# A gated recurrence's factor computed without the square of a, and its exchanged copy by GpSimd

## Chip, cores, metric

One Trainium2 chip; the program runs on one of its cores. The metric is device microseconds of one execution, as the median of the runs shown.

## What is computed

Two layers of a hybrid backbone over 256 context and 256 latent tokens of width 2048. Each layer projects the tokens to 7184 columns and feeds three groups: a bidirectional gated recurrence (RG-LRU, 1024 channels), windowed attention with 8 heads, and a bidirectional state space scan (SSD, 16 heads). A projection back to 2048 columns and a residual close the layer. The change lies in the recurrence:

```python
def rglru_scan(xc, w_a, b_a, w_x, b_x, lam, h0, reverse):
    ...
    r = jax.nn.sigmoid(jnp.einsum('blhi,hij->blhj', xb, w_a.astype(jnp.float32)).reshape(bsz, L, W) + b_a)
    i = jax.nn.sigmoid(jnp.einsum('blhi,hij->blhj', xb, w_x.astype(jnp.float32)).reshape(bsz, L, W) + b_x)
    log_a = -LRU_C * r * jax.nn.softplus(-lam.astype(jnp.float32))
    a = jnp.exp(log_a)
    b = jnp.sqrt(-jnp.expm1(2.0 * log_a)) * (i * xf)
    ...
    h = linear_scan(a, b, reverse)
```

It runs once per direction. The gates' weights are block diagonal: 16 blocks of 64 channels.

## The kernel before

**Work of the matmuls.** Activations lie with channels on the 128 partitions and the 512 tokens along the row. A projection to 128 columns is one PSUM tile `acc` of 128 x 512, summed over 16 blocks of the input. So that fp32 accuracy is kept, every weight piece is split into `hi` and `lo` (`blocks`, L228): a piece of 256 KB comes by DMA into one of five `raw` buffers, ScalarE copies it to `hi` (L237), VectorE subtracts to get `lo` (L238), and each of its four blocks gives three matmuls (`mm3`, L242). There are four buffers for `hi` and four for `lo`. TensorE's order of work is written by hand; the other engines' order is set by a scheduler at build time, and each engine works its own queue strictly in that order.

**Order of a layer.** Projections run in the order of `body` (L72): columns for the state space scan first, then in turn for the eight channel tiles of the recurrence `lx` (its input, always 512 tokens) and `lg` (its gate; 512 tokens in layer 0, only the 256 latent ones in layer 1), then the rest. After each projection its follow-up work is started as a generator; parts of it that need TensorE are put between the matmuls once a clock that counts matmul time has gone on by the amount in the table `WAIT`. While the tiles of the recurrence are projected, the state space scan (`ssd_core`; L1119 to L1191) also runs.

**One channel tile of the recurrence** (`lru_x`, L688). ScalarE and VectorE do a convolution of four taps over `acc` into `xc` (L460, three times L466). The gates' matmuls work on quadrants of 64 x 64 and need the two halves of `xc` also exchanged: ScalarE makes the copy `xsw`, two halves of 64 x 512 (L694). Then, for each direction: eight small matmuls into two PSUM tiles `mx` (four of these are shared by everybody); ScalarE takes the two gates out by Tanh (L712), giving `tr` and `ti`; Tanh of log a into `tl` (L717); Exp, which gives a (L718); Square of a into `la2` (L720). VectorE multiplies (a squared + 1) into `tl` (L721) and makes (ti + 1) x xc (L722). With both directions done ScalarE takes the root of `tl` in one operation of 128 x 1024 (L724), before which it loads another activation table. GpSimd multiplies it into `ti` (L727), VectorE runs the recurrences (L730; L733 and L735 backward), GpSimd adds the directions (L739) and multiplies by the output gate (L749), and the result is stored to DRAM. Since tanh(log a) = (a^2 - 1)/(a^2 + 1), the product of L721 is a^2 - 1.

`xc`, `la2`, the gate `lgt` and other roles share the four buffers of tag `td`.

Of the kernel before, what the change touches and what calls it, by code (L numbers as in the profile page):

```python
# [10 lines left out]
AF = mybir.ActivationFunctionType  # L11
ALU = mybir.AluOpType
AX = mybir.AxisListType

P = 128
# [124 lines left out]
class Kernel:  # L140
# [526 lines left out]
    def lru_begin(self, l):  # L667
        nc = self.nc
        o = PARAMS["lam"][0]
        ng = self.t([P, 16], "nlam", 1)  # L670
        nc.vector.tensor_scalar(out=ng, in0=self.prm[:, o:o + 16], scalar1=-1.0, scalar2=None, op0=ALU.mult)
        sp = self.softplus(ng, 16, "lsp")
        self.s4 = self.t([P, 16], "s4", 1)
        nc.vector.tensor_scalar(out=self.s4, in0=sp, scalar1=-4.0, scalar2=None, op0=ALU.mult)
        self.gb = self.t([P, 32], "gbh", 1)
        o = PARAMS["gab"][0]
        nc.vector.tensor_scalar(out=self.gb, in0=self.prm[:, o:o + 32], scalar1=0.5, scalar2=None, op0=ALU.mult)
        self.gws = [self.gate_weights(l, 0)]
        self.lruD = self.dram([8, P, 512], "lruD")
# [8 lines left out]
    def lru_x(self, l, m, px):  # L688
        nc = self.nc
        xc = self.t([P, 512], "xc")  # L690
        self.conv(xc, px, lambda tap: self.par("lcw", tap * 8 + m), self.par("lcb", m), 2)
        xs = self.t([P, 512], "xsw")
        for r, o in ((0, 64), (64, 0)):
            nc.scalar.activation(out=xs[r:r + 64], in_=xc[o:o + 64], func=AF.Copy)  # L694
        gw = self.gws.pop(0)
        if m < 7:
            self.gws.append(self.gate_weights(l, m + 1))
        yield self.wait("lx")
        ab = []
        tl = self.t([P, 2, 512], "ltl", 1)  # L700
        for d in range(2):
            if d:
                yield self.wait("lx2")
            th = []
            pg = [self.mx() for _ in range(2)]
            for r, c in ((0, 0), (64, 64), (0, 64), (64, 0)):
                x = xc if r == c else xs
                self.mm(pg[r // 64][c:c + 64], gw[r:r + 64, int(r != c), 2 * d + r // 64], x[r:r + 64], pos=(r, c),
                        side=4)
            for g in range(2):  # L710
                t = self.t([P, 512], f"lt{g}", 2)
                nc.scalar.activation(out=t, in_=pg[g], func=AF.Tanh, scale=0.5,  # L712
                                     bias=self.gb[:, 16 * g + 8 * d + m:16 * g + 8 * d + m + 1])
                th.append(t)
            tr, ti = th
            s4 = self.s4[:, 8 * d + m:8 * d + m + 1]
            nc.scalar.activation(out=tl[:, d], in_=tr, func=AF.Tanh, scale=s4, bias=s4)  # L717
            nc.scalar.activation(out=tr, in_=tr, func=AF.Exp, scale=s4, bias=s4)  # L718
            a2 = self.t([P, 512], "la2", 1)
            nc.scalar.activation(out=a2, in_=tr, func=AF.Square)  # L720
            nc.vector.scalar_tensor_tensor(out=tl[:, d], in0=a2, scalar=1.0, in1=tl[:, d], op0=ALU.add, op1=ALU.mult)  # L721
            nc.vector.scalar_tensor_tensor(out=ti, in0=ti, scalar=1.0, in1=xc, op0=ALU.add, op1=ALU.mult)  # L722
            ab.append((tr, ti))
        nc.scalar.activation(out=tl, in_=tl, func=AF.Sqrt, scale=-0.0625, bias=self.eps["s"])  # L724
        hs = []
        for d, (tr, ti) in enumerate(ab):
            nc.gpsimd.tensor_tensor(out=ti, in0=ti, in1=tl[:, d], op=ALU.mult)  # L727
            h = self.t([P, 512], f"lh{d}", 2)
            if d == 0:
                nc.vector.tensor_tensor_scan(out=h, data0=tr, data1=ti, initial=0.0, op0=ALU.mult, op1=ALU.add)  # L730
            else:
                r = lambda x, s: x[:, s:s + 256][:, ::-1]
                nc.vector.tensor_tensor_scan(out=r(h, 0), data0=r(tr, 0), data1=r(ti, 0), initial=0.0, op0=ALU.mult,  # L733
                                             op1=ALU.add)
                nc.vector.tensor_tensor_scan(out=r(h, C), data0=r(tr, C), data1=r(ti, C), initial=h[:, 0:1],  # L735
                                             op0=ALU.mult, op1=ALU.add)
            hs.append(h)
        s = C if l else 0
        nc.gpsimd.tensor_tensor(out=hs[0][:, s:], in0=hs[0][:, s:], in1=hs[1][:, s:], op=ALU.add)  # L739
        self.lru_h[m] = hs[0]  # L740
# [536 lines left out]
```

## Time and profile before

| what | value |
|---|---|
| runs | 1833.20, 1832.97, 1830.13 us; median 1832.97 |
| profiled execution, own time | 1829.47 us |
| its span | 1827.5 us |
| busy: TensorE | 1765.5 us (97%) |
| busy: VectorE | 1407.4 us (77%) |
| busy: ScalarE | 973.3 us (53%) |
| busy: GpSimd | 214.7 us (12%) |
| granted clock of TensorE, mean | 0.991 |

The span runs from the first to the last instruction in the trace; the time holds 2 us more around it. PE is TensorE, PEld its weight loads, DVE is VectorE, ACT is ScalarE, POOL is GpSimd. The shares are means over the whole program: ScalarE's work is concentrated in the two stretches of the recurrence, 225 to 495 us (layer 0) and 1290 to 1495 us (layer 1).

### The profile page before, as it was taken

The page shows a single profiled execution, that of the slowest core. Times are in us where ns is not written, and L with a number is a line of the kernel's source. Part 1 is how long each engine was busy: PE and PEld are TensorE (multiplying, and loading weights), DVE is VectorE, ACT ScalarE, POOL GpSimd, SP SyncE. Part 2 cuts the span into 40 slices and gives each one's busy share as a digit, 9 for nine tenths or more (in the row PEclk, how much of TensorE's full clock was granted, in tenths as well). Part 3 has the DMA queues.
Part 4 walks back from the last instruction along what each step waited for, and adds up shares of the span by engine and source line. Part 5 has one row for each costly group of instructions (what it writes and reads, how often), then busy time and mean ns, then how long its engine had stood idle before and what let it go on. Part 6 is the DMA issues. An engine that isn't in the chain of part 4 may idle for free.

```text
span 1827.5 us, 30170 instructions
## 1 busy us (share of the span) xinstructions
PE 1765.5 (97%) x10522; PEld 1453.4 (80%) x10522; DVE 1407.4 (77%) x3117; ACT 973.3 (53%) x1798; POOL 214.7 (12%) x179
## 2 busy tenths in 40 slices
PE   7999999999999999999999999999989999999999
PEld 4677876667778778887888887888767788999999
DVE  4447769898899778899999536877688785788665
ACT  4324578688523354556232235545688863678443
POOL 0000111111210021211000021010021130121000
PEclk9999999999999999999999999999999999999999
DMA  9982333434675545556766433455243564554655
GB/s 364 389 292 66 124 104 102 122 122 146 220 221 180 179 150 185 178 182 221 238 220 222 158 122 107 133 185 168 96 138 107 179 214 142 182 178 155 217 185 179
DMA packets 186344, 322.99 MB, mean 177 GB/s; under 512 B 19121, under 2 KB 44625, under 8 KB 185553
## 3 DMA queue, kind: packets, MB, share of 16 engines
q1 hardware_dynamic: 186192, 321.09, 54.2%
q8 instruction: 82, 1.34, 0.3%
q14 instruction: 70, 0.57, 0.1%
HBM read 310.38 MB, written 10.63 MB: 176 GB/s over the span
## 4 chain that ended last, share of the span: by engine, by line
PE 72%; DVE 9%; issue 7%; ACT 7%; DMA 3%; POOL 1%; SPq 0%; ACTq 0%; DVEq 0%; POOLq 0%
PE acc L174 55%; PE mx L174 13%; PE ada L174 3%; DVE lo L238 2%; PE mx L170 2%; DMA bc<-acsD 1%; ACT hi L237 1%; DVE ada L380 1%; DVE araw L380 1%; ACT lt L712 1%; DVE lh L730 1%; DMA araw<-in_adaw_dram 1%; DVE xc L466 1%; DVE ee L1165 1%; ACT ww L1167 1%
## 5 line engine op out<-in xcount | busy, mean ns | idle before, releaser
L174 PE MATMUL acc<-u,hi 128*128 128x512 f32 (+1 forms) x4800 | 1277.4, 355 | 3.9 <-ACT u L452 3.1
L174 PEld LDWEIGHTS acc<-u,hi 128*128 128x128 f32 x4800 | 837.1, 190 | 149.0 <-issue 32.6
L174 PE MATMUL acc<-u,lo 128*128 128x512 f32 (+1 forms) x2400 | 842.4, 351 | 6.9 <-DVE lo L238 6.7
L237 ACT ACTIVATE hi<-raw 128x512 fp32r<-128x512 f32 x640 | 397.8, 628 | 544.4 <-PE acc L174 420.8
L238 DVE TENSOR_TENSOR lo<-raw,hi 128x512 fp32r<-128x512 f32 x640 | 457.9, 718 | 184.6 <-ACT hi L237 172.7
L174 PEld LDWEIGHTS acc<-u,lo 128*128 128x128 f32 x2400 | 455.5, 190 | 71.9 <-DVE lo L238 11.7
L380 DVE SCALAR_TENSOR_TENSOR araw<-araw,adac 128x512 f32<-128x512 f32 x256 | 183.2, 716 | 6.9 <-DMA araw<-in_adaw_dram 4.1
L380 DVE SCALAR_TENSOR_TENSOR ada<-araw,adac 128x512 f32<-128x512 f32 x192 | 141.6, 738 | 13.0 <-DMA adac<-condD 7.0
L174 PE MATMUL mx<-u,hi 128*128 128x512 f32 (+1 forms) x320 | 99.7, 395 | 0.0
L1077 DVE SCALAR_TENSOR_TENSOR X<-acc,mod,X 128x256 f32<-128x256 f32 x144 | 65.0, 478 | 39.5 <-PE acc L174 39.4
L727 POOL TENSOR_TENSOR lt<-lt,ltl 128x512 f32<-128x512 f32 x32 | 45.5, 1443 | 326.2 <-ACT ltl L724 305.3
L868 POOL TENSOR_SCALAR prob<-prob,qrs 128x512 f32<-128x512 f32 (+1 forms) x48 | 58.2, 1227 | 214.7 <-ACT hi L237 124.7
L427 POOL TENSOR_TENSOR ssq<-ssq,sq 128x512 f32<-128x512 f32 (+1 forms) x26 | 34.1, 1312 | 308.0 <-ACT sq L423 308.0
L174 PEld LDWEIGHTS mx<-u,hi 128*128 128x128 f32 x320 | 56.6, 191 | 14.2 <-issue 4.6
L174 PE MATMUL mx<-u,lo 128*128 128x512 f32 (+1 forms) x160 | 61.0, 382 | 0.0
L511 POOL TENSOR_SCALAR X<-xs,prm 128x512 f32<-128x512 f32 (+1 forms) x16 | 15.4, 968 | 361.6 <-DVE xs L489 357.1
L174 PE MATMUL mx<-xc,gw 64*64 64x512 f32 x128 | 40.8, 619 | 8.9 <-ACT lt L712 5.9
L423 ACT ACTIVATE sq<-X 128x256 f32<-128x256 f32 (+1 forms) x44 | 18.8, 452 | 54.8 <-DVE X L654 53.1
L1165 DVE SCALAR_TENSOR_TENSOR ee<-bc,nacs,ee 128x128 f32<-128x128 f32 x96 | 35.9, 427 | 15.0 <-DMA bc<-acsD 9.6
L771 POOL TENSOR_TENSOR qw<-qw,cst 128x256 f32<-128x256 f32 x20 | 23.1, 1156 | 197.7 <-DVE rt L770 169.7
L712 ACT ACTIVATE lt<-mx,gbh 128x512 f32<-128x512 f32 x64 | 42.0, 674 | 4.1 <-PE mx L174 4.0
L1164 ACT ACTIVATE ee<-bc,nacs 128x128 f32<-128x128 f32 x96 | 30.9, 390 | 17.7 <-DMA bc<-acsD 17.7
(240 smaller groups left out, 1953.1 us busy)
## 6 DMA issues: line engine op xcount, KB each, us to landing
raw<-in_w_in_dram SPq DMA_DIRECT2D x448, 256.0 KB, 2.8
araw<-in_adaw_dram SPq DMA_DIRECT2D x256, 256.0 KB, 3.0
raw<-in_w_out_dram SPq DMA_DIRECT2D x192, 256.0 KB, 3.0
ar<-in_ada_dram SPq DMA_DIRECT2D x84, 256.0 KB, 5.4
bc<-acsD SPq DMA_DIRECT2D x48, 256.0 KB, 3.7
ar<-in_ada_dram SPq DMA_DIRECT2D x22, 512.0 KB, 6.9
adac<-condD SPq DMA_DIRECT2D x28, 256.0 KB, 4.5
gw<-in_gates_dram SPq DMA_DIRECT2D x16, 256.0 KB, 2.9
```

The costliest lines, as they stand in the source:

```text
L170: self.nc.tensor.transpose(out=out, in_=lhsT, identity=rhs)
L174: self.nc.tensor.matmul(out=out, lhsT=lhsT, rhs=rhs, start=start, stop=stop, **kw)
L237: nc.scalar.activation(out=hi, in_=part, func=AF.Copy)
L238: nc.vector.tensor_tensor(out=lo, in0=part, in1=hi.bitcast(F32), op=ALU.subtract)
L380: i = nc.vector.scalar_tensor_tensor(out=o, in0=raw, scalar=1.0, in1=row[c].rearrange("p t x -> p (t x)"), op0=ALU.mult, op1=ALU.mult, acc ...
L427: nc.gpsimd.tensor_tensor(out=self.ssq[0], in0=self.ssq[0], in1=sq, op=ALU.add)
L712: nc.scalar.activation(out=t, in_=pg[g], func=AF.Tanh, scale=0.5, bias=self.gb[:, 16 * g + 8 * d + m:16 * g + 8 * d + m + 1])
L727: nc.gpsimd.tensor_tensor(out=ti, in0=ti, in1=tl[:, d], op=ALU.mult)
L868: nc.gpsimd.tensor_scalar(out=pr[j], in0=pr[j], scalar1=rs[:, j:j + 1], scalar2=1.0, op0=ALU.mult, op1=ALU.mult)
L1077: nc.vector.scalar_tensor_tensor(out=x[:, s], in0=acc[:, s.start - w0:s.stop - w0], scalar=mod[:, 2 * KT + m, c:c + 1], in1=x[:, s], op0=A ...
L1164: nc.scalar.activation(out=e[:, j], in_=bcs[0][:, j], func=AF.Identity, bias=k.nacs[:, f:f + 1])
L1165: nc.vector.scalar_tensor_tensor(out=e[:, j], in0=bcs[1][:, j], scalar=k.nacs[:, r:r + 1], in1=e[:, j], op0=ALU.add, op1=ALU.min)
```

## The change

tanh(log a / 2) = (a - 1)/(a + 1), and the root of (1 - a)/(1 + a) times (1 + a) is the root of 1 - a^2. So the Tanh takes half the exponent (a second scale `s2`, computed once per layer), the Square goes, and the factor (a + 1) is multiplied in by VectorE behind the root instead of (a^2 + 1) before it. The exchanged copy `xsw` is made by GpSimd, as a multiplication by 1.0 twice.

```diff
@@ lru_begin
         nc.vector.tensor_scalar(out=self.s4, in0=sp, scalar1=-4.0, scalar2=None, op0=ALU.mult)
+        self.s2 = self.t([P, 16], "s2", 1)
+        nc.vector.tensor_scalar(out=self.s2, in0=sp, scalar1=-2.0, scalar2=None, op0=ALU.mult)
@@ lru_x
         for r, o in ((0, 64), (64, 0)):
-            nc.scalar.activation(out=xs[r:r + 64], in_=xc[o:o + 64], func=AF.Copy)
+            nc.gpsimd.tensor_scalar(out=xs[r:r + 64], in0=xc[o:o + 64], scalar1=1.0, scalar2=1.0, op0=ALU.mult,
+                                    op1=ALU.mult)
...
-            s4 = self.s4[:, 8 * d + m:8 * d + m + 1]
-            nc.scalar.activation(out=tl[:, d], in_=tr, func=AF.Tanh, scale=s4, bias=s4)
+            s4, s2 = (x[:, 8 * d + m:8 * d + m + 1] for x in (self.s4, self.s2))
+            nc.scalar.activation(out=tl[:, d], in_=tr, func=AF.Tanh, scale=s2, bias=s2)
             nc.scalar.activation(out=tr, in_=tr, func=AF.Exp, scale=s4, bias=s4)
-            a2 = self.t([P, 512], "la2", 1)
-            nc.scalar.activation(out=a2, in_=tr, func=AF.Square)
-            nc.vector.scalar_tensor_tensor(out=tl[:, d], in0=a2, scalar=1.0, in1=tl[:, d], op0=ALU.add, op1=ALU.mult)
...
         for d, (tr, ti) in enumerate(ab):
+            nc.vector.scalar_tensor_tensor(out=tl[:, d], in0=tr, scalar=1.0, in1=tl[:, d], op0=ALU.add, op1=ALU.mult)
             nc.gpsimd.tensor_tensor(out=ti, in0=ti, in1=tl[:, d], op=ALU.mult)
```

TensorE's order of work is the same instruction for instruction. The scheduler moves the work of the other engines within the two stretches of the recurrence; three places follow. The line numbers are each kernel's own: in the changed one L696 is the copy, L715 the gates' Tanh, L720 Tanh, L721 Exp, L724 the root, L727 the new product, L728 GpSimd's multiplication, L731, L734 and L736 the recurrences, L740 and L750 GpSimd's addition and gate.

First excerpt: VectorE, first channel tile of layer 0, around the products. Before:

```order
L722 SCALAR_TENSOR_TENSOR lt_527_2548<-lt_527_2548,xc_2428 128x512
L721 SCALAR_TENSOR_TENSOR ltl_2539<-la_528_2552,ltl_2539 128x512
L722 SCALAR_TENSOR_TENSOR lt_535_2576<-lt_535_2576,xc_2428 128x512
L238 TENSOR_TENSOR lo_2679<-raw_2676,hi_2678 128x512
L1119 TENSOR_TENSOR xw_2625<-X_1804,wst_2360 128x512
L721 SCALAR_TENSOR_TENSOR ltl_2539<-la_536_2580,ltl_2539 128x512
L238 TENSOR_TENSOR lo_2697<-raw_2694,hi_2696 128x512
L730 SCALAR_TENSOR_TENSOR lh_537_2586<-lt_526_2546,lt_527_2548 128x512
```

Changed:

```order
L722 SCALAR_TENSOR_TENSOR lt_528_2550<-lt_528_2550,xc_2430 128x512
L722 SCALAR_TENSOR_TENSOR lt_535_2575<-lt_535_2575,xc_2430 128x512
L727 SCALAR_TENSOR_TENSOR ltl_2541<-lt_527_2548,ltl_2541 128x512
L727 SCALAR_TENSOR_TENSOR ltl_2541<-lt_534_2573,ltl_2541 128x512
L238 TENSOR_TENSOR lo_2677<-raw_2674,hi_2676 128x512
L238 TENSOR_TENSOR lo_2695<-raw_2692,hi_2694 128x512
L731 SCALAR_TENSOR_TENSOR lh_536_2583<-lt_527_2548,lt_528_2550 128x512
```

The two products now stand side by side, ahead of two splits, and both read what the root has written.

Second excerpt: GpSimd, from the first to the second channel tile of layer 0. Before:

```order
L727 TENSOR_TENSOR lt_535_2576<-lt_535_2576,ltl_2539 128x512
L739 TENSOR_TENSOR lh_537_2586<-lh_537_2586,lh_538_2589 128x512
L749 TENSOR_TENSOR lh_537_2586<-lh_537_2586,lgt_2517 128x512
L727 TENSOR_TENSOR lt_588_2818<-lt_588_2818,ltl_2809 128x512
L727 TENSOR_TENSOR lt_593_2840<-lt_593_2840,ltl_2809 128x512
```

Changed:

```order
L728 TENSOR_TENSOR lt_535_2575<-lt_535_2575,ltl_2541 128x512
L740 TENSOR_TENSOR lh_536_2583<-lh_536_2583,lh_537_2587 128x512
L750 TENSOR_TENSOR lh_536_2583<-lh_536_2583,lgt_2519 128x512
L696 TENSOR_SCALAR xsw_2648<-xc_2643 64x512 x2
L728 TENSOR_TENSOR lt_587_2816<-lt_587_2816,ltl_2807 128x512
L728 TENSOR_TENSOR lt_591_2835<-lt_591_2835,ltl_2807 128x512
```

The copy for the next tile stands behind the last two operations of the tile before. It is so in all of layer 0; in layer 1 it stands between L728 and L740 of the tile before.

Third excerpt: ScalarE, fourth channel tile of layer 1, from the last gate's Tanh. Before:

```order
L712 ACTIVATE lt_3010_13555<-mx_13548,gbh_11799 128x512
L720 ACTIVATE la_3003_13531<-lt_3001_13525 128x512
L1128 ACTIVATE H_13576<-mx_13574 128x512
L718 ACTIVATE lt_3009_13553<-lt_3009_13553,s_2638_11797 128x512
L237 ACTIVATE hi_13659<-raw_13657 128x512
L237 ACTIVATE hi_13681<-raw_13679 128x512
L720 ACTIVATE la_3011_13559<-lt_3009_13553 128x512
L237 ACTIVATE hi_13699<-raw_13697 128x512
L237 ACTIVATE hi_13723<-raw_13721 128x512
L724 ACT_TABLE_LOAD
L724 ACTIVATE ltl_13518<-ltl_13518,epss_92 128x1024
L460 ACTIVATE xc_13586<-acc_13447,prm_1005 128x512
```

Changed:

```order
L715 ACTIVATE lt_2989_13512<-mx_13505,gbh_11771 128x512
L720 ACTIVATE ltl_13478<-lt_2988_13510,s_2624_11769 128x512
L1129 ACTIVATE H_13532<-mx_13530 128x512
L721 ACTIVATE lt_2988_13510<-lt_2988_13510,s_2623_11767 128x512
L724 ACT_TABLE_LOAD
L724 ACTIVATE ltl_13478<-ltl_13478,epss_92 128x1024
L237 ACTIVATE hi_13615<-raw_13613 128x512
L460 ACTIVATE xc_13542<-acc_13407,prm_1005 128x512
L237 ACTIVATE hi_13637<-raw_13635 128x512
L237 ACTIVATE hi_13655<-raw_13653 128x512
L237 ACTIVATE hi_13679<-raw_13677 128x512
```

The four splits that stood ahead of the root now stand behind it.

## Rows read from the trace of the kernel before

**Rows 1.** Windows: length, PE, PEld, DVE, ACT, POOL busy (count), clock, DMA, GB/s.
```profile
225.00:495.00 270.00, 256.61 (x1320) 188.06 (x1319) 227.13 (x444) 203.50 (x383) 44.82 (x32) 0.97 0.42 133
1290.00:1495.00 205.00, 190.49 (x1242) 148.59 (x1235) 170.03 (x298) 166.51 (x292) 42.29 (x35) 0.99 0.45 141
```

**Rows 2.** PE's waits, 225 to 495, then 1290 to 1495: us, times, longest.
```profile
PE mx L174 <- DVE ee L1171: 4.5, 2, 3.1
PE mx L174 <- ACT lt L712: 3.1, 1, 3.1
PE mx L174 <- ACT xsw L694: 2.3, 1, 2.3
...
PE mx L174 <- ACT lt L712: 9.7, 7, 4.1
PE acc L174 <- DVE lo L238: 4.7, 5, 1.6
```

**Rows 3.** Windows behind three waits of PE.
```profile
339.00:344.00 5.00, 4.17 (x13) 2.30 (x14) 4.36 (x10) 5.00 (x10) 0.00 (x0) 0.66 0.53 157
442.00:446.20 4.20, 4.13 (x31) 3.00 (x32) 4.20 (x10) 4.11 (x8) 0.00 (x0) 0.59 0.50 156
1343.00:1347.30 4.30, 3.19 (x6) 1.91 (x7) 4.19 (x10) 4.30 (x8) 0.00 (x0) 0.60 0.31 106
```

**Rows 4.** Tile lt and line L724: durations min/median/max; one wait (us, times).
```profile
L712 ACT ACTIVATE lt<-mx,gbh x64: 666/672/692, 241.5 to 1474.9; 128x512 f32<-128x512 f32 x64
L717 ACT ACTIVATE ltl<-lt,s x32: 800/813/821, 242.2 to 1474.2; 128x512 f32<-128x512 f32 x32
L718 ACT ACTIVATE lt<-lt,s x32: 802/808/824, 243.5 to 1476.0; 128x512 f32<-128x512 f32 x32
...
L720 ACT ACTIVATE la<-lt x32: 617/632/637, 244.3 to 1478.0; 128x512 f32<-128x512 f32 x32
...
  DVE ltl L721: 5.0, 8
...
L724 ACT ACT_TABLE_LOAD  x16: 1283/1283/1283, 249.2 to 1480.0; - x16
L724 ACT ACTIVATE ltl<-ltl,epss x16: 1151/1152/1155, 250.5 to 1481.3; 128x1024 f32<-128x1024 f32 x16
```

**Rows 5.** Timeline of POOL, DVE and ACT, 429 to 442: start us, us.
```profile
429.71 1.30 POOL L749 TENSOR_TENSOR lh<-lh,lgt 128x512 f32<-128x512 f32 x1
...
429.70 1.45 DVE L1165 SCALAR_TENSOR_TENSOR ee<-bc,nacs,ee 128x128 f32<-128x128 f32 x1
...
435.60 0.74 DVE L466 SCALAR_TENSOR_TENSOR xc<-acc,prm,xc 128x510 f32<-128x510 f32 x1
...
438.72 0.35 DVE L1165 SCALAR_TENSOR_TENSOR ee<-bc,nacs,ee 128x128 f32<-128x128 f32 x1
...
440.38 1.28 ACT L694 ACTIVATE xsw<-xc 64x512 f32<-64x512 f32 x2
```

**Rows 6.** ACT's waits for the copy: layer 0's stretch, then layer 1's.
```profile
ACT xsw L694 <- DVE xc L466: 14.2, 5, 4.2
...
ACT xsw L694 <- DVE lh L730: 8.2, 4, 3.7
ACT xsw L694 <- DVE xc L466: 7.6, 2, 4.7
```

**Rows 7.** Timeline of ACT and PE, 1389 to 1396.
```profile
1389.26 1.29 ACT L694 ACTIVATE xsw<-xc 64x512 f32<-64x512 f32 x2 [4.71 <-DVE xc L466]
...
1393.91 1.07 PE L174 MATMUL mx<-xc,gw 64*64 64x512 f32 x2 [0.95 <-ACT lt L712]
...
1395.39 0.64 PE L174 MATMUL mx<-xc,gw 64*64 64x512 f32 x1 [0.41 <-ACT lt L712]
```

**Rows 8.** Line L511, GpSimd's one-input operation: durations min/median/max.
```profile
L511 POOL TENSOR_SCALAR X<-xs,prm x16: 481/698/1584, 183.3 to 1268.5; 128x512 f32<-128x512 f32 x8, 128x256 f32<-128x256 f32 x8
```

**Rows 9.** Chain of waits, one piece: start us, us, what, how many.
```profile
1493.61 11.42 PE acc L174 x93
```

## Prediction, before the result was known

> **What bounds the kernel now.** Read first the windows over the two stretches in which the eight channel tiles of the recurrence are worked off, one per layer [rows 1]. TensorE is busy 256.61 of 270 us and 190.49 of 205 us, so it bounds both; it loses 13.4 us in the first and 14.5 us in the second. VectorE is at 84% and 83%, ScalarE at 75% and 81%, GpSimd at 17% and 21%. Nothing in the change alters TensorE's instructions or their order; the time can only fall where TensorE waits, by at most these 27.9 us and what its clock loses after a wait.
>
> Next, who ends TensorE's waits there [rows 2]. In the first stretch ScalarE ends 3.1 us (L712, the gates' Tanh, which empties the PSUM tile that the next matmul needs) and 2.3 us (L694, the exchanged copy itself); VectorE's L1171 ends 4.5 us. In the second, L712 ends 9.7 us in 7 waits and the split's L238 on VectorE 4.7 us. So 15.1 us end on ScalarE, and ScalarE is late because it works its queue in order.
>
> Then the clock [rows 3]: in the three short windows behind the waits that end at 339.8, 441.1 and 1344.1 us the granted clock is 0.66, 0.59 and 0.60, a mix of the 2.4 and the 1.2 GHz level. What is lost is (1 - 0.66) x 5.0 = 1.7 us, (1 - 0.59) x 4.2 = 1.7 us and (1 - 0.60) x 4.3 = 1.7 us, 5.1 us in all, each behind a wait that ScalarE ended.
>
> **The change, part by part.** *Off ScalarE: the Square.* 32 of L720 at 632 ns [rows 4] are 20.2 us. *Off ScalarE: the copies.* 32 of L694; the row shows two in 1.28 us [rows 5], so 16 pairs are 20.5 us. Beyond their own time they stand in ScalarE's queue and wait for the convolution: 14.2 us in the first stretch, 8.2 and 7.6 us in the second [rows 6], 30 us in which everything behind them stands still. Together 71 us leave ScalarE's queue, 4.4 us per channel tile.
>
> What of it reaches TensorE I price wait by wait. The wait of 2.3 us: the convolution ends at 435.60 + 0.74 = 436.3 us, but the copy starts at 440.38 [rows 5], because ScalarE's queue has other work ahead of it. GpSimd's last piece of work before, L749, ends at 429.71 + 1.30 = 431.0 us [rows 5]; there the copy could start at 436.3 us. All of the 2.3 us goes. The waits of 0.95 us before 1393.91 and 0.4 us behind it: ScalarE stood idle 4.71 us for a convolution and then copied for 1.29 us [rows 7], all ahead of L712 in its queue; these 6.0 us exceed the wait, so 1.4 us goes. Of the remaining 3.1 + 9.7 - 1.4 = 11.4 us I cannot follow each chain; I take two thirds, 7.6 us, because 4.4 us leave the queue per tile while a wait is 1.3 us in the mean (9.7 / 7), but other late work (transfers, VectorE) stands behind some. Sum: -11.3 us; the bounds are -3.7 us (the two waits that I followed) and -15.1 us (all).
>
> *Clock.* The drop behind 441.1 us goes with its wait; of the other two I take one: -3.4 us, bounds -1.7 and -5.1 us.
>
> *On GpSimd: 32 one-input operations of 64 x 512.* The trace of before has no such shape. The nearest row is L511, also a one-input TENSOR_SCALAR: median 698 ns, longest 1584 ns [rows 8]. I take 0.70 us, as 512 columns per partition stay the same; the long end is one that waited. 22.4 us in all, on an engine that is idle 80% of the time. GpSimd's queue is passed too: in layer 0 the copy for tile m+1 stands behind L739 and L749 of tile m, in layer 1 ahead of them (the second excerpt of the order). In the case at 436.3 us it finds GpSimd free; the delay of L739 in layer 1 ends in a store that nobody waits for at once. Taken at nothing; the cover is the time between the copy and the gate matmuls.
>
> *Both engines at once.* L1165, normally 0.35 us, takes 1.45 us at 429.70 us, while L749 runs on GpSimd [rows 5]. So a GpSimd operation can hold a VectorE operation off for its whole length. The Trainium skill, page "SBUF — State Buffer", section "🔬 SBUF: two separate sides", states the rule: the port pair that GpSimd and VectorE share is an exclusive lock, and a VectorE operation with two SBUF inputs blocks for the whole GpSimd instruction. By that rule all 22.4 us could be added to VectorE, and the sum below would turn from gain to loss; this is the third rival. From rows: GpSimd already works 44.82 + 42.29 = 87.1 us in these stretches [rows 1], and VectorE's waits of 4.5 and 4.7 us [rows 2] are what TensorE feels with that. 22.4 / 87.1 = 26% more GpSimd work, so 26% of 9.2 us: +2.4 us; bounds 0 and +22.4 us.
>
> *The product moved behind the square root.* The count of VectorE's operations stays the same (32 of L721 go, 32 come, and one tiny multiplication per layer for the factor -2). Before, it waited 5.0 us in all for the Square [rows 4]; now it waits for the Sqrt with its table load, 1.283 + 1.152 us [rows 4], and VectorE's queue stands behind it. In the first excerpt of the order the split's L238 stands behind it, but this needs its hi, which ScalarE makes only after the Sqrt. Where nothing else stands between, VectorE was going to be idle anyway. I take 0, bounds 0 and the second rival's price. The la2 tile also gives back half of the buffers it shared with xc and lgt: 0, for no wait of TensorE names them.
>
> **Sum.** -11.3 - 3.4 + 2.4 = -12.3 us. The profiled execution took 1829.47 us, so 1817.2; the median of the runs, 1832.97, stands 3.5 us above it, so the forecast is 1820.7 us (0.7% faster). About 0.2%, 3.7 us, is what a measurement of this kernel can tell from no change.
>
> **The rivals.** *First: VectorE takes ScalarE's place.* It is busier than ScalarE in both stretches [rows 1], and the convolution that the copies waited for 30 us is its work [rows 6]: if gates come late because conv comes late, the waits stay and only change their name. Against it: the waits are named ScalarE's, and one was followed to its start. Then only 2.3 + 1.7 us are gained and 2.4 us lost: about 1832 us, no difference.
>
> *Second: ScalarE's burst without a split (slower).* The order of the changed kernel packs the eight gate activations, table load and Sqrt of a tile tightly (third excerpt): between a tile's first gate Tanh and its Sqrt stood 2, 2, 2, 2, 4, 3, 1, 2 (layer 0) and 4, 3, 4, 4, 5, 5, 4, 5 (layer 1) operations of L237; now 0, 1, 1, 1, 2, 1, 0, 0 and 2, 0, 2, 0, 2, 1, 1, 1. A burst lasts 4 x 0.672 + 2 x 0.813 + 2 x 0.808 + 1.283 + 1.152 = 8.4 us [rows 4]. TensorE lives on four hi/lo buffers of 12 matmuls each. At 256 columns it took 11.42 us for 93 [rows 9], 1.47 us a buffer, 5.9 us for four. So where a burst falls on a half-width tile of layer 1 (L238 already ends 4.7 us there [rows 2]) 2.5 us are missing. It decides where no or one L237 stands in the burst: two of layer 1 with none, 2 x 2.5; three with one, 3 x (2.5 - 1.47) = 3.1; two clock drops of 1.7 each: +11.5 us. Layer 1 then gains nothing, layer 0 keeps three quarters of its 5.4 us and 3.4 us of clock, less 2.4: -5.1. Net +6.4: 1839 us. For it speaks the order; against it, that buffers are full when ScalarE is early, and that hi is made in a row right after the Sqrt.
>
> *Third: the lock (slower).* All 22.4 us of GpSimd's new work hold VectorE, and VectorE, with 16% idle, hands it to TensorE: +22.4 - 11.3 - 3.4 = +7.7, 1841 us. Against it: 87.1 us of such work now cost TensorE at most 9.2 us.
>
> **How the numbers follow.** Forecast 0.58; first rival 0.17, second 0.15, third 0.07, the rest 0.03. The likeliest case has its own range: from all 15.1 us, all 5.1 us, no lock and the 4.7 us that L238 ends and that ScalarE feeds (-24.9: 1808) to the two followed waits and one clock drop less the lock (-3.0: 1830). The range, 1807 to 1840, takes in the first two rivals. Faster 0.59, the same 0.18, slower 0.23: the forecast's upper edge and the first rival give the same, the second and third slower.
>
> **What would show it.** In the profile after: L720 and the copies gone from ScalarE, its busy time lower by 41 us; the copies on GpSimd near 0.7 us; TensorE's waits that L712 ends in the two stretches down from 12.8 us to about 4; no clock drop near 441 us. Right in sum but wrong in step: L712's waits gone, the same total under L1171 or L238 (first rival). Second rival: L238 ends more than 10 us in layer 1's stretch, with VectorE idle for L237. Third: L238 or L1165 well over their present mean, copies well over 0.7 us. The forecast is wrong if TensorE's idle time in both stretches together stays above 24 us.

## The result, and the profile after

The changed kernel takes 1851.13 us (median of 4 runs, 1848.61 to 1855.83), the kernel before, on the same chip, 1831.55 us (4 runs). The ratio is 1.0113, 95% interval 1.0099 to 1.0126: slower by 1.1%. The forecast was 1820.7 us with a range of 1807 to 1840, so the sign was wrong and the time lies outside the range. The profiled execution of the changed kernel took 1855.83 us (span 1853.8), that of the kernel before 1829.47 us (span 1827.5). One run of the kernel e7 below took 9419.78 us, in the slow state, and is left out of its median and its ratio.

First the page of the changed kernel, busy time by engine, and its mean granted clock:

```profile
PE 1781.5 (96%) x10522; PEld 1461.6 (79%) x10522; DVE 1422.0 (77%) x3119; ACT 940.8 (51%) x1734; POOL 250.9 (14%) x211
...
core 0: 1853.8 us, clock 0.983
```

ScalarE (ACT) is relieved as planned, 973.3 to 940.8 us, and GpSimd (POOL) has more to do. But the span grew by 26.3 us, and it can be split. TensorE's time without work, span less busy, went from 1827.5 - 1765.5 = 62.0 to 1853.8 - 1781.5 = 72.3 us: 10.3 us more. The same 10522 matmuls took 16.0 us more, and nearly all of that is the clock: (1 - 0.983) x 1853.8 = 31.5 us against (1 - 0.991) x 1827.5 = 16.4, that is 15.1 us. (This pair of executions is 26.3 us apart, the medians 19.6, as the profiled execution is the longest of the changed kernel's four; the shares of the loss are read from the pair, its size from the medians. The pair also makes the clock's share look large: the changed kernel's four executions have a mean clock of 0.983, those of the kernel before in the experiments below one of 0.989 to 0.990, and by these some 12 of the 19.6 us would be clock, an estimate.)

Next the windows over the two stretches of the recurrence, which answer to [rows 1], and three short ones behind waits, which answer to [rows 3]. The columns are those of [rows 1], the clock third from the end.

```profile
225.00:495.00 270.00, 253.33 (x1294) 183.53 (x1294) 225.51 (x438) 184.01 (x347) 61.47 (x46) 0.96 0.40 129
1290.00:1495.00 205.00, 186.69 (x1100) 141.15 (x1102) 161.46 (x269) 135.18 (x234) 48.02 (x42) 0.94 0.38 121
...
1437.90:1445.00 7.10, 7.07 (x17) 3.40 (x18) 4.93 (x15) 5.66 (x13) 0.00 (x0) 0.52 0.46 148
1454.00:1459.00 5.00, 4.71 (x20) 3.44 (x22) 5.00 (x8) 3.20 (x7) 1.95 (x2) 0.66 0.39 136
1481.80:1486.00 4.20, 4.14 (x22) 4.14 (x23) 4.20 (x8) 1.40 (x3) 1.15 (x1) 0.59 0.53 178
```

TensorE now loses 16.7 and 18.3 us, 35.0 us in place of 27.9; the prediction called itself wrong above 24. In layer 1's 205 us it gets through 1100 matmuls where it did 1242. The last three windows follow waits of 1.70, 1.75 and 1.98 us: the granted clock is 0.52, 0.66 and 0.59, a mix of the 1.2 and 2.4 GHz levels, as behind the waits of [rows 3]. Up to the end of each of these waits it is 1.00.

Where the time is lost shows when the start of each of TensorE's matmuls is compared with that of its counterpart before. Until 237 us the two traces are 0.4 us apart; at 451 us, after layer 0's recurrence, the changed kernel is 6 us late; it loses 4 us up to 1260 us, and between 1290 and 1507 us, in layer 1's recurrence, another 17. From there to the end nothing is added.

TensorE's waits in these stretches (225 to 495 us, then 1290 to 1530 us), for [rows 2]: who released it, us in all, times, longest.

```profile
PE mx L174 <- DVE ee L1172: 8.5, 5, 4.4
PE mx L174 <- ACT lt L715: 3.2, 1, 3.2
...
PE mx L174 <- POOL xsw L696: 1.8, 1, 1.8
...
PE acc L174 <- DVE lo L238: 9.1, 6, 2.0
PE mx L174 <- ACT lt L715: 8.6, 4, 4.7
PE acc L174 <- ACT hi L237: 3.3, 3, 1.7
```

The waits that the gates' Tanh ends, 3.1 + 9.7 us before, are 3.2 + 8.6 us (L715 is what L712 was): nothing is gained there. What grew are the waits for VectorE's ee in layer 0 (4.5 to 8.5 us) and for the split's two halves in layer 1: L238 from 4.7 to 9.1 us, and L237, which ended none of TensorE's waits there before, 3.3 us.

One such wait, in the timeline of the changed kernel (start us, us, engine, operation; in brackets the idle time before it and what ended that), ScalarE first, then VectorE, GpSimd and TensorE:

```profile
1383.38 0.61 ACT L237 ACTIVATE hi<-raw 128x512 fp32r<-128x512 f32 x1
...
1385.77 1.25 ACT L715 ACTIVATE lt<-mx,gbh 128x512 f32<-128x512 f32 x2
1386.90 0.81 ACT L720 ACTIVATE ltl<-lt,s 128x512 f32<-128x512 f32 x1
...
1391.60 1.28 ACT L724 ACT_TABLE_LOAD   x1
1392.90 1.15 ACT L724 ACTIVATE ltl<-ltl,epss 128x1024 f32<-128x1024 f32 x1
1393.95 0.62 ACT L237 ACTIVATE hi<-raw 128x512 fp32r<-128x512 f32 x1
...
1394.08 1.29 DVE L727 SCALAR_TENSOR_TENSOR ltl<-lt,ltl 128x512 f32<-128x512 f32 x2 [2.46 <-ACT ltl L724]
1395.29 1.76 DVE L238 TENSOR_TENSOR lo<-raw,hi 128x512 fp32r<-128x512 f32 x1
...
1394.85 3.35 POOL L728 TENSOR_TENSOR lt<-lt,ltl 128x512 f32<-128x512 f32 x2 [13.69 <-DVE ltl L727]
...
1397.11 0.39 PE L174 MATMUL acc<-u,lo 128*128 128x256 f32 x1 [1.10 <-DVE lo L238]
```

From 1383.38 to 1393.95 us, 10.6 us, ScalarE makes no high half (hi); 8.3 us of it are gates, table load and root in one piece, 1385.77 to 1394.05 us. The hi of 1393.95 is done at 1394.57. Then VectorE's lo comes late twice over: the two products L727, which waited 2.46 us for the root, stand ahead of it and end at 1395.37, and the lo itself takes 1.76 us in place of its usual 0.69, while GpSimd's L728, which these products released, runs. TensorE has used up its buffers and waits 1.10 us.

The Trainium skill, page "SBUF — State Buffer", section "🔬 SBUF: two separate sides", says that of a VectorE operation with two SBUF inputs and a GpSimd operation the one that starts first keeps the shared ports and the other waits. The 1.76 us agree, L728 having started 0.44 us earlier. Over the whole trace it is not so each time: of 640 lo operations 132 overlap some GpSimd work, and the median of these is 694 ns, but 57 of them took over 0.9 us. Before it was 37 of 96. So the new order has also moved GpSimd's products in among the splits: 20 of the 57 lie beside L728, where 10 lay beside L727.

In layer 0 the same order does its harm in another place. First the kernel before, ScalarE then VectorE, then the changed kernel, with GpSimd last:

```profile
275.21 1.27 ACT L1164 ACTIVATE ee<-bc,nacs 128x128 f32<-128x128 f32 x4
...
282.21 1.15 ACT L724 ACTIVATE ltl<-ltl,epss 128x1024 f32<-128x1024 f32 x1
...
275.97 1.13 DVE L1165 SCALAR_TENSOR_TENSOR ee<-bc,nacs,ee 128x128 f32<-128x128 f32 x4
...
281.44 0.68 DVE L1171 TENSOR_TENSOR ee<-ee,ww 128x512 f32<-128x512 f32 x1
```

```profile
275.22 1.16 ACT L724 ACTIVATE ltl<-ltl,epss 128x1024 f32<-128x1024 f32 x1
276.28 1.27 ACT L1165 ACTIVATE ee<-bc,nacs 128x128 f32<-128x128 f32 x4
...
276.41 1.29 DVE L727 SCALAR_TENSOR_TENSOR ltl<-lt,ltl 128x512 f32<-128x512 f32 x2 [1.65 <-ACT ltl L724]
277.62 3.21 DVE L1166 SCALAR_TENSOR_TENSOR ee<-bc,nacs,ee 128x128 f32<-128x128 f32 x4
...
281.54 1.21 DVE L731 TENSOR_TENSOR_SCAN lh<-lt,lt 128x512 f32<-128x512 f32 x1
...
283.71 0.68 DVE L734 TENSOR_TENSOR_SCAN lh<-lt,lt 128x256 f32<-128x256 f32 x1
...
286.69 0.68 DVE L1172 TENSOR_TENSOR ee<-ee,ww 128x512 f32<-128x512 f32 x1
...
277.25 2.90 POOL L728 TENSOR_TENSOR lt<-lt,ltl 128x512 f32<-128x512 f32 x2 [14.20 <-DVE ltl L727]
```

Before, the scan's ee and ww steps went ahead and the root came last, at 282.21. Now the root goes first. VectorE's four ee steps come behind its products and take 3.21 us in place of 1.13, with GpSimd's product beside them, and two of the recurrence's own scans, L731 and L734, also stand ahead now; the ee that TensorE needs starts at 286.69 in place of 281.44 us, and TensorE waits 4.4 us for it.

The copies themselves, in the tile view (durations in ns, shortest, median, longest):

```profile
L696 POOL TENSOR_SCALAR xsw<-xc x32: 612/886/2692, 234.4 to 1487.9; 64x512 f32<-64x512 f32 x32
```

### The profile page after: what moved, and what is told of

The parts are those of the page before. It is cut to its first block, busy times and chain, and to the rows that moved or that the text cites. A ratio compares the mean times of both kernels' runs of the same rounds, so it can differ in the third digit from the quotient of the medians.

```text
span 1853.8 us, 30143 instructions
## 1 busy us (share of the span) xinstructions
PE 1781.5 (96%) x10522; PEld 1461.6 (79%) x10522; DVE 1422.0 (77%) x3119; ACT 940.8 (51%) x1734; POOL 250.9 (14%) x211
## 4 chain that ended last, share of the span: by engine, by line
PE 79%; DVE 8%; DMA 5%; ACT 5%; issue 2%; POOL 1%; SPq 0%; DVEq 0%; ACTq 0%; POOLq 0%
PE acc L174 62%; PE mx L174 13%; PE ada L174 2%; DVE lo L238 2%; DMA bc<-acsD 2%; PE mx L170 2%; DVE ada L380 1%; DVE ee L1166 1%; ACT lt L715 1%; DVE araw L380 1%; DMA ar<-in_ada_dram 1%; ACT ww L1168 1%; DMA araw<-in_adaw_dram 1%; DMA X<-in_xT_dram 1%; DMA raw<-in_w_in_dram 0%
## 5 line engine op out<-in xcount | busy, mean ns | idle before, releaser
L237 ACT ACTIVATE hi<-raw 128x512 fp32r<-128x512 f32 x640 | 397.8, 628 | 594.5 <-PE acc L174 455.0
L238 DVE TENSOR_TENSOR lo<-raw,hi 128x512 fp32r<-128x512 f32 x640 | 475.1, 746 | 175.5 <-ACT hi L237 166.3
L380 DVE SCALAR_TENSOR_TENSOR ada<-araw,adac 128x512 f32<-128x512 f32 x192 | 141.1, 735 | 11.5 <-DMA adac<-condD 7.2
L728 POOL TENSOR_TENSOR lt<-lt,ltl 128x512 f32<-128x512 f32 x32 | 51.8, 1638 | 245.6 <-DVE ltl L727 231.9
L511 POOL TENSOR_SCALAR X<-xs,prm 128x512 f32<-128x512 f32 (+1 forms) x16 | 15.4, 965 | 363.6 <-DVE xs L489 359.1
L715 ACT ACTIVATE lt<-mx,gbh 128x512 f32<-128x512 f32 x64 | 41.9, 674 | 17.6 <-PE mx L174 17.5
```

The source lines that it names most:

```text
L237: nc.scalar.activation(out=hi, in_=part, func=AF.Copy)
L238: nc.vector.tensor_tensor(out=lo, in0=part, in1=hi.bitcast(F32), op=ALU.subtract)
L380: i = nc.vector.scalar_tensor_tensor(out=o, in0=raw, scalar=1.0, in1=row[c].rearrange("p t x -> p (t x)"), op0=ALU.mult, op1=ALU.mult, acc ...
```

## The experiments

Four theories were set against each other. **Burst:** without the Square, the root needs nothing of VectorE, the scheduler sees it ready at once and packs it onto the gates, so splits and ee come late. **Root wait:** the product moved behind the root makes VectorE's queue stand still. **Lock:** GpSimd's copies hold VectorE's operations. **Order as such:** something else in the new order. Below, "splits" are the operations of L237 between a tile's first gate Tanh and its root, in the kernel's order of instructions, summed over layer 0's and layer 1's eight tiles: 18 and 34 before, 6 and 9 in the changed kernel. Each difference is against the kernel before as it ran beside that kernel; its median was 1830.51 us for e1, e2, e3 and e6, 1831.28 for e4, e7, e8 and e9, and 1831.77 for e11, e12, e14 and e16.

**e1, the factor alone.** To the changed kernel:

```diff
-            nc.gpsimd.tensor_scalar(out=xs[r:r + 64], in0=xc[o:o + 64], scalar1=1.0, scalar2=1.0, op0=ALU.mult,
-                                    op1=ALU.mult)
+            nc.scalar.activation(out=xs[r:r + 64], in_=xc[o:o + 64], func=AF.Copy)
```

> The change's factor alone: no Square, product behind the root, but the exchanged copies stay on ScalarE. Before is 1831.5 us and the changed kernel 1851.1 (+20). Burst theory (gate activations and root packed, the high halves of the splits late): the factor carries the loss, +12 to +22 us over before. Root-wait theory (VectorE's queue stands in L727 for the root): the same, +12 to +22. Lock theory (GpSimd's copies hold VectorE's two-input operations): the loss goes with the copies, within 4 us of before.

Measured: 1848.6 us, ratio 1.01 (1.0075 to 1.0124), +18.1 us. The factor carries most of the loss.

**e2, the copies alone.** To the kernel before:

```diff
-            nc.scalar.activation(out=xs[r:r + 64], in_=xc[o:o + 64], func=AF.Copy)
+            nc.gpsimd.tensor_scalar(out=xs[r:r + 64], in0=xc[o:o + 64], scalar1=1.0, scalar2=1.0, op0=ALU.mult,
+                                    op1=ALU.mult)
```

> The other half alone: the kernel before with its 32 half-tile copies on GpSimd in place of ScalarE, Square and product as they were. Burst theory and root-wait theory: between 5 us faster and 3 us slower than before (20 us of ScalarE's work leaves, and GpSimd's copies meet few of VectorE's operations). Lock theory: +12 to +20 us.

Measured: 1835.55 us (10 runs), ratio 1.002 (1.0002 to 1.0039), that is +3.7 us with an interval of 0.4 to 7.1. That is just above the range that the first two theories gave. So the copies do cost something, if little, although 18 us of ScalarE's busy time are gone (973.3 to 955.2). The lock as the main cause falls. The ratios of e1 and e2 give 18.3 + 3.7 = 22.0 us, against 20.7 by the changed kernel's ratio: the halves add up.

**e3, the product ahead of the root.** To the changed kernel:

```diff
             nc.vector.scalar_tensor_tensor(out=ti, in0=ti, scalar=1.0, in1=xc, op0=ALU.add, op1=ALU.mult)
+            nc.vector.scalar_tensor_tensor(out=ti, in0=tr, scalar=1.0, in1=ti, op0=ALU.add, op1=ALU.mult)
...
-            nc.vector.scalar_tensor_tensor(out=tl[:, d], in0=tr, scalar=1.0, in1=tl[:, d], op0=ALU.add, op1=ALU.mult)
```

> The changed kernel, but VectorE multiplies (a+1) into the gated input ahead of the root, so that no VectorE operation waits for the root (21.2 us of such waits in the changed kernel); the same count of instructions, the same order on ScalarE. Root-wait theory: most of the loss goes, within 5 us of before. Burst theory: the gates' burst on ScalarE is as packed as in the changed kernel, and +12 us or more over before stays. Lock theory: +15 us or more stays.

Measured: 1845.13 us, ratio 1.0077 (1.0053 to 1.0102), +14.6 us. Some 5 us of the loss go (6.6 by the ratios), the larger part stays, as the burst theory has it; the root wait alone is not the cause. TensorE's waits in e3, 1290 to 1530 us:

```profile
PE mx L174 <- ACT lt L715: 9.6, 5, 5.5
PE acc L174 <- ACT hi L237: 5.1, 4, 2.0
PE acc L174 <- DVE lo L238: 4.0, 6, 0.9
```

With no product in the way the lo follows its hi at once, so L238's 9.1 us fall to 4.0; but the hi itself is late, 5.1 us.

**e6, the root held behind VectorE.** To the changed kernel, 16 one-column operations in all; the value of the bias is the same, as the input counts times zero:

```diff
+        e1 = self.t([P, 1], "e1", 2)
+        nc.vector.scalar_tensor_tensor(out=e1, in0=ti[:, :1], scalar=0.0, in1=self.eps["s"], op0=ALU.mult, op1=ALU.add)
-        nc.scalar.activation(out=tl, in_=tl, func=AF.Sqrt, scale=-0.0625, bias=self.eps["s"])
+        nc.scalar.activation(out=tl, in_=tl, func=AF.Sqrt, scale=-0.0625, bias=e1)
```

> The changed kernel with the root's bias made by a one-column VectorE operation that reads the second direction's gated input, so that the scheduler sees the root ready only after VectorE's turn and puts more splits between a tile's first gate activation and its root (per tile 1,1,1,1,2,2,1,1 and 2,2,2,1,3,3,2,2 in place of 0,1,1,1,2,1,0,0 and 2,0,2,0,2,1,1,1; the kernel before had 2,2,2,2,4,3,1,2 and 4,3,4,4,5,5,4,5). 16 small operations are added on VectorE. Burst theory: a third to a half of the loss goes, +8 to +14 us over before. Root-wait theory: the root comes later and VectorE waits longer for it, +20 to +26 us. Lock theory: +18 to +22 us.

Measured: 1842.38 us, ratio 1.0063 (1.0039 to 1.0087), +11.9 us. Splits of 10 and 17 in place of 6 and 9 go with 8 us less. VectorE goes on waiting for the root behind which its product stands:

```profile
DVE ltl L729 <- ACT ltl L726: 20.0, 15, 2.5
```

**e4, e3 without GpSimd's copies.** To e3:

```diff
-            nc.gpsimd.tensor_scalar(out=xs[r:r + 64], in0=xc[o:o + 64], scalar1=1.0, scalar2=1.0, op0=ALU.mult,
-                                    op1=ALU.mult)
+            nc.scalar.activation(out=xs[r:r + 64], in_=xc[o:o + 64], func=AF.Copy)
```

> The early product of the run e3 with the exchanged copies back on ScalarE: the splits between gate activations and root are as few as in the changed kernel, no VectorE operation waits for the root, GpSimd has no copy. If the costs of the copies (+3.7 us), of the wait for the root (6.5) and of the packed burst add up: +9 to +13 us over before. If the wait for the root and the copies were all of it: within 4 us of before.

Measured: 1842.02 us, ratio 1.0062 (1.0037 to 1.0086), +10.7 us. With copies and root wait both taken away, 11 us are left; the burst theory puts them down to the packed order, and e8 and e14 below test that.

**e7, e3 and e6 together.** To e3:

```diff
-        nc.scalar.activation(out=tl, in_=tl, func=AF.Sqrt, scale=-0.0625, bias=self.eps["s"])
+        nc.scalar.activation(out=tl, in_=tl, func=AF.Sqrt, scale=-0.0625, bias=e1)
```

(with e6's operation ahead of it).

> e3 and e6 in one: product ahead of the root, and the root held behind VectorE's turn by the one-column bias; copies on GpSimd. If burst and wait for the root are separate costs: +14.6 of e3 less the 9 that e6 gave back, +4 to +8 us over before. If both runs took away the same cost: +11 to +14.

Measured: 1829.58 us (9 runs), ratio 0.9999 (0.9987 to 1.0012). The whole loss is gone, with all of the change's work still off ScalarE and the copies still on GpSimd. It is more than was expected: 5 and 8 us alone, 20 together. The trace shows why the two do not simply add: e7 has 13 and 32 splits ahead of its roots, where e6 has 10 and 17, for the same one-column operation here reads ti behind the second product, which needs ScalarE's Exp. So e7 holds the root longer than e6 does. TensorE's waits in e7, 225 to 530 and 1290 to 1530 us:

```profile
PE mx L174 <- DVE ee L1174: 2.7, 3, 1.6
...
PE mx L174 <- ACT lt L715: 7.5, 6, 3.5
PE acc L174 <- DVE lo L238: 4.7, 7, 0.9
```

The waits for ee in layer 0 and for lo in layer 1 are back at or under those of before, and L237 ends none in layer 1.

**e8, e7 with the copies on ScalarE.** To e7:

```diff
-            nc.gpsimd.tensor_scalar(out=xs[r:r + 64], in0=xc[o:o + 64], scalar1=1.0, scalar2=1.0, op0=ALU.mult,
-                                    op1=ALU.mult)
+            nc.scalar.activation(out=xs[r:r + 64], in_=xc[o:o + 64], func=AF.Copy)
```

> e7 with the copies on ScalarE. Here the scheduler puts 1,2,2,1,3,2,1,1 and 4,3,5,2,6,6,4,3 splits between a tile's first gate activation and its root, about as many as before the change (2,2,2,2,4,3,1,2 and 4,3,4,4,5,5,4,5), with 21 us of ScalarE's Square gone. Burst theory: the loss is gone, from 4 us faster to 3 us slower than before. A loss from another source (the new order as such): +8 us or more.

Measured: 1829.77 us (10 runs), ratio 0.9988 (0.9972 to 1.0005). The loss is gone. But with nearly as many splits as before (13 and 33) and without the Square it is not faster either.

**e14, the control.** To e8:

```diff
-        nc.vector.scalar_tensor_tensor(out=e1, in0=ti[:, :1], scalar=0.0, in1=self.eps["s"], op0=ALU.mult, op1=ALU.add)
+        nc.vector.scalar_tensor_tensor(out=e1, in0=ab[0][1][:, :1], scalar=0.0, in1=self.eps["s"], op0=ALU.mult, op1=ALU.add)
```

> A control for e8: the same 16 one-column operations and the same bias operand, but they read the first direction's gated input instead of the second's, which is ready long before; the splits between gate activations and root stay at e4's 0,1,1,1,2,1,0,0 and 2,0,2,0,2,1,1,1. Burst theory: as e4, +8 to +13 us over before. If the added operations or the operand gave e8 its time and not the place of the splits: within 3 us of before.

Measured: 1846.0 us, ratio 1.0071 (1.0052 to 1.0091), +14.2 us by the medians, a little above the expected range, and 13.0 by the ratio, at its upper end. The same 16 operations with the splits where e4 has them (6 and 9) have about e4's loss. So it is the place of the root in the order, and what moves with it, that decides between 1829.8 and 1846.0 us. TensorE's waits in e14, 225 to 530 and 1290 to 1530 us:

```profile
PE mx L174 <- DVE ee L1173: 6.8, 2, 5.7
...
PE mx L174 <- ACT lt L714: 11.5, 4, 5.2
PE acc L174 <- DVE lo L238: 4.2, 5, 0.9
```

**e9, both factors ahead of the root on VectorE.** To e1, a version without Square and without a product behind the root:

```diff
+            for _ in range(2):
+                nc.vector.scalar_tensor_tensor(out=tl[:, d], in0=tr, scalar=1.0, in1=tl[:, d], op0=ALU.add, op1=ALU.mult)
             nc.vector.scalar_tensor_tensor(out=ti, in0=ti, scalar=1.0, in1=xc, op0=ALU.add, op1=ALU.mult)
...
-            nc.vector.scalar_tensor_tensor(out=tl[:, d], in0=tr, scalar=1.0, in1=tl[:, d], op0=ALU.add, op1=ALU.mult)
```

> Without the square of a on ScalarE, but with VectorE multiplying by (a+1) twice ahead of the root (32 more operations of some 0.7 us, 22 us of VectorE), copies on ScalarE. Splits between gate activation and root: 2,2,2,2,3,3,1,2 and 4,3,5,3,6,6,5,4, as before. Burst theory: no loss from ScalarE; VectorE's 22 us cost between 0 and 8 us. If removing the Square itself were the loss: +10 us or more.

Measured: 1823.86 us (8 runs), ratio 0.9962 (0.9949 to 0.9975), 7 us faster than before: better than expected: VectorE's added operations show no cost. ScalarE's timeline in e9, at the tile shown above for the changed kernel:

```profile
1366.46 1.24 ACT L714 ACTIVATE lt<-mx,gbh 128x512 f32<-128x512 f32 x2
...
1369.49 0.63 ACT L237 ACTIVATE hi<-raw 128x512 fp32r<-128x512 f32 x1
...
1370.67 1.15 ACT L237 ACTIVATE hi<-raw 128x512 fp32r<-128x512 f32 x2
1371.84 1.28 ACT L725 ACT_TABLE_LOAD   x1
1373.14 1.15 ACT L725 ACTIVATE ltl<-ltl,epss 128x1024 f32<-128x1024 f32 x1
```

Three splits stand ahead of the table load that had none. But before had 18 and 34 splits and e9 has 17 and 36, so the count does not explain why e9 is faster than before; by the starts of the same matmuls in the two traces, one execution each, 2.8 us of its gain lie in layer 0's recurrence, 3.9 between the two layers' recurrences and 1.3 in layer 1's.

**e16, dead work on VectorE.** To e8; the result is read by the one-column operation alone, times zero:

```diff
+        a2 = self.t([P, 512], "la2", 1)
+        nc.vector.scalar_tensor_tensor(out=a2, in0=tr, scalar=1.0, in1=ti, op0=ALU.add, op1=ALU.mult)
-        nc.vector.scalar_tensor_tensor(out=e1, in0=ti[:, :1], scalar=0.0, in1=self.eps["s"], op0=ALU.mult, op1=ALU.add)
+        nc.vector.scalar_tensor_tensor(out=e1, in0=a2[:, :1], scalar=0.0, in1=self.eps["s"], op0=ALU.mult, op1=ALU.add)
```

> e8 with one more VectorE operation per tile (128x512, its result used by nothing but the one-column operation) ahead of the root: 16 times some 0.7 us of dead work, 11 us of VectorE. Splits between gate activation and root rise from 13 to 19 in layer 0 and from 33 to 36 in layer 1 (e9: 17 and 36). Burst theory: as e9, 3 to 9 us faster than before although VectorE does more. If e9 was fast for another reason (where its product stands): e8's time or up to 5 us above it, from 1 us faster to 4 us slower than before.

Measured: 1822.02 us (6 runs), ratio 0.994 (0.9923 to 0.9958), the lowest median of all: 10 us under before, a little more than was expected, and 8 under e8, by adding 11 us of useless work that holds the root back. It speaks for the order, since nothing was taken from any engine. Its lead over e9 is not clear of the noise. ScalarE's timeline in e16 ahead of a root shows what such an order looks like:

```profile
1371.40 0.63 ACT L237 ACTIVATE hi<-raw 128x512 fp32r<-128x512 f32 x1 [0.78 <-PE acc L174]
1372.85 0.63 ACT L237 ACTIVATE hi<-raw 128x512 fp32r<-128x512 f32 x1 [0.81 <-PE acc L174]
1373.49 1.28 ACT L728 ACT_TABLE_LOAD   x1
1374.79 1.15 ACT L728 ACTIVATE ltl<-ltl,e 128x1024 f32<-128x1024 f32 x1
```

It is the same tile once more. ScalarE waits for TensorE to free a buffer before it can make the next hi, so at this root TensorE has the work that the hi buffers hold. This row shows the order, not where the gain lies: by the starts of the same matmuls, of the 9.4 us that the trace of e16 gains on that of e8, 5.0 lie in layer 0's recurrence, where the splits rose from 13 to 19, and 0.7 in layer 1's.

**e11, dead work on ScalarE.** To e8:

```diff
+        a2 = self.t([P, 512], "la2", 1)
+        nc.scalar.activation(out=a2, in_=tr, func=AF.Square)
-        nc.vector.scalar_tensor_tensor(out=e1, in0=ti[:, :1], scalar=0.0, in1=self.eps["s"], op0=ALU.mult, op1=ALU.add)
+        nc.vector.scalar_tensor_tensor(out=e1, in0=a2[:, :1], scalar=0.0, in1=self.eps["s"], op0=ALU.mult, op1=ALU.add)
```

> e8 with a Square of the second direction's factor on ScalarE ahead of the root, its result used by nothing but the one-column operation: 16 times some 0.6 us, 10 us of ScalarE; splits 2,2,2,2,3,2,1,1 and 4,3,4,3,5,5,3,3, in number as e8's. If ScalarE's work costs time where the splits are spread (e9 has 21 us less of it than before and is 7 us faster): 2 to 6 us over e8, that is 1 to 5 us slower than before. If only the place of the splits counts: e8's time, within 2 us.

Measured: 1831.49 us (12 runs), ratio 0.9994 (0.9982 to 1.0007), e8's time within what can be told. Eight more us of ScalarE's busy time (958.1 to 966.3) cost nothing measurable here, with 15 and 30 splits in place of 13 and 33.

**e12, e9 with the copies on GpSimd.** To e9:

```diff
-            nc.scalar.activation(out=xs[r:r + 64], in_=xc[o:o + 64], func=AF.Copy)
+            nc.gpsimd.tensor_scalar(out=xs[r:r + 64], in0=xc[o:o + 64], scalar1=1.0, scalar2=1.0, op0=ALU.mult,
+                                    op1=ALU.mult)
```

> e9, the fastest so far (7 us under before), with the exchanged copies on GpSimd as the change has them: 20 us of ScalarE's work gone too, splits as in e9 (2,2,2,2,3,3,1,2 and 4,3,5,3,6,5,5,4). If ScalarE's work still counts there: 2 to 6 us under e9. If the copies cost what e2 showed (+3.7): 2 to 6 us over e9, 1 to 5 us under before.

Measured: 1828.19 us (12 runs), ratio 0.9978 (0.9966 to 0.999): some 3 to 4 us over e9, each taken against its own before, as e2 had it; the two intervals just overlap.

All in one table; TensorE's waits are those of each trace in 225 to 530 us (ee) and 1290 to 1530 us (lo + hi; gates' Tanh), in us. Kernels with 6 to 10 and 9 to 17 splits lose 10.7 to 19.6 us, those with 13 to 19 and 30 to 36 lie between -9.8 and +5.0; within either group the count does not set the order of the times.

| kernel | splits, layer 0 / 1 | against before (medians), us | ee | lo + hi | Tanh |
|---|---|---|---|---|---|
| before | 18 / 34 | 0 | 4.5 | 4.7 | 9.7 |
| changed | 6 / 9 | +19.6 | 8.5 | 9.1 + 3.3 | 8.6 |
| e1 | 6 / 10 | +18.1 | 9.3 | 8.0 + 4.8 | 9.0 |
| e3 | 6 / 9 | +14.6 | 7.3 | 4.0 + 5.1 | 9.6 |
| e14 | 6 / 9 | +14.2 | 6.8 | 4.2 + 1.4 | 11.5 |
| e4 | 6 / 9 | +10.7 | 9.6 | 4.2 + 1.4 | 10.9 |
| e6 | 10 / 17 | +11.9 | 9.7 | 5.1 + 0.2 | 10.5 |
| e7 | 13 / 32 | -1.7 | 2.7 | 4.7 | 7.5 |
| e8 | 13 / 33 | -1.5 | 4.9 | 3.5 | 8.4 |
| e9 | 17 / 36 | -7.4 | 2.8 | 3.1 | 7.2 |
| e16 | 19 / 36 | -9.8 | 1.9 | 2.8 | 8.3 |
| e11 | 15 / 30 | -0.3 | 3.9 | 4.2 + 0.7 | 9.6 |
| e12 | 17 / 35 | -3.6 | 4.8 | 4.9 | 4.5 |
| e2 | 18 / 34 | +5.0 | 6.8 | 4.3 | 8.2 |

## Why the prediction was wrong

**The step that failed is the first term of the sum, "I take two thirds, 7.6 us, because 4.4 us leave the queue per tile", with the product behind the root, of which it says "I take 0".** Both priced work by its duration and not by the order that it leaves behind. The first term, -11.3 us in the sum, measured -1.5 us, the second some 5 to 7 us in place of 0, and the packed order itself, which stood only among the rivals, some 11 us (e4).

- *ScalarE's waits, -11.3 us.* Measured in the profiled pair: 12.8 us of L712's waits became 3.2 + 8.6 = 11.8, and the copy's 2.3 us became 1.8, now ended by GpSimd: -1.5 us. Ahead of the longest of these waits, 4.7 us, ScalarE of the changed kernel was idle for 3.53 us, waiting for a transfer that the ee step needs:

```profile
1382.20 1.28 ACT L1165 ACTIVATE ee<-bc,nacs 128x128 f32<-128x128 f32 x4 [3.53 <-DMA bc<-acsD]
```

  There a shorter queue gains nothing. Of the kernels in the table only e12 halves layer 1's Tanh waits, and it is 3 to 4 us behind e9. That ScalarE's busy time is not the price is what e11 says too, where 8 us more of it cost nothing measurable.
- *Clock, -3.4 us.* Measured +15.1 us in the profiled pair. The waits that were to vanish stayed, new ones came, and behind three waits of 1.70 to 1.98 us the granted clock was 0.52 to 0.66.
- *Lock, +2.4 us.* The one term of about the right size: by the ratios the copies on GpSimd in place of ScalarE cost 3.7 us (e2), 2.4 (changed kernel against e1), 2.7 (e3 against e4), 2.0 (e7 against e8) and 2.9 (e12 against e9), of which only e2's is clear of the noise by its own interval. Its reason is not settled: VectorE's busy time rises by 9.7 us in e2 (1407.4 to 1417.1), as with a lock, but each of these differences holds the copies' cost on GpSimd together with whatever ScalarE's relief is worth. The row of L696 shows 612 ns at the shortest, but 886 in the median, in place of the 0.70 us taken from [rows 8].
- *The product behind the root, 0.* The argument "this needs its hi, which ScalarE makes only after the Sqrt" holds for the next lo, but the products stand ahead of it with 1.29 us and release GpSimd's product into it (1394.08 to 1397.05 us above). VectorE waited 21.2 us for the root in all; two pairs with the same or nearly the same splits put the price at 5.0 us (changed kernel against e3) and 7.4 us (e1 against e4). The 13 us between e6 and e7 are no such price, as e7 also has more splits ahead of its roots.
- *The second rival came nearest to the cause.* Its count of splits was the right view and its test, over 10 us in layer 1's stretch, was nearly met by the two halves together: 7.1 us end on L238 and 2.6 on L237 from 1290 to 1495 us, and 9.1 and 3.3, 12.4 in all, up to 1530, as the same work now ends later; L238 alone stays under 10. It was given 0.15 and priced at +6.4 us net. Its own price for layer 1, +11.5, was nearer than any other to the 17 lost there; the error is in what it set against that: layer 0 was to gain 5.1 us, and lost 6, and there the waits for ee grew by 4.0 us, as the root, its products and the scans go ahead of the ee and ww steps, which the count of splits does not show. The objection that "buffers are full when ScalarE is early" is the state of the tile shown for e16, not of that shown for the changed kernel.
- *The first rival* (VectorE takes ScalarE's place) is not what sets the time: e9 and e16 load VectorE more and are faster. But part of what it foresaw is there, for the waits that VectorE's lo and ee end did grow.

What stays open: how much of the loss is due to the late splits, how much to the late ee steps and how much to GpSimd's products beside VectorE's lo, as all three change with the place of the root (lo operations of over 0.9 us: 37 before, 57 in the changed kernel, 48 in e1, 44 in e14, 36 in e8); what makes e9 and e16 faster than before at nearly the same count of splits; and whether a hand-written place for the root, without dead work, gains as much as e16. None of these was tried.

## What to carry to other kernels

Before pricing an operation taken off an in-order engine, look at what it had kept apart: removing a dependency makes its successor ready earlier, and a scheduler that fills by readiness will put that successor ahead of work that the bounding engine is waiting for. A piece without a deadline (here table load and root, which with the gates made 8 us in one piece) can be worth holding behind the work that feeds that engine, by an order or, as here, by a dependency that costs next to nothing (e14 to e8, 16 us); e9, with no dead work in it, is the version to keep from this study (1823.86 us, ratio 0.9962), though why it beats the kernel before is not shown. And where the bounding engine is TensorE, a new wait can cost as much again in clock as in time (15.1 and 10.3 us in the pair here; for e1 against before 5.7 and 11.3).

## What was not expected of the hardware

- The clock took the larger part of the loss in the profiled pair, 15.1 us against 10.3 us of idle time: behind waits of 1.70 to 1.98 us the granted clock stood at 0.52 to 0.66 in the windows shown.
- GpSimd's one-input copy of 64 x 512 lasted 612 ns at the shortest, yet 2692 ns at the longest; beside its product L728 operations of VectorE that started later took two or three times as long (0.69 to 1.76 us for a lo, 1.13 to 3.21 us for four ee steps), while 75 of the 132 lo operations that overlapped GpSimd's work took no more than 0.9 us.
- Adding 11 us of work to VectorE, the second-busiest engine, came with a kernel 8 us faster (e16 against e8).
